# Banded attention: the products of weights and values of the two heads of a pair, one head after the other or alternately

## The chip, the cores and the metric

The kernel runs on 1 core of one Trainium2 chip. The metric is the device time of one execution in microseconds (us); for the kernel before it is given as the median of 3 runs, and every comparison with it is made on the same chip.

## The reference

The program is one block of a first kind (a chunked mLSTM and a "stick-breaking" attention, gates, an MLP) and two layers of a second kind. Each of these two layers computes an HGRN2 recurrence over eight heads of 128 and, beside it, banded attention over sixteen heads of 64 with two key/value heads; the two results, gated, are multiplied by an output matrix. All data are float32; the sequence has 512 rows, the model 1024 columns. What the change touches is the end of the banded attention:

```python
    s = jnp.einsum('bnqkgd,bnskd->bnkgqs', qb, kw).astype(jnp.float32) * ATT_SCALE
    ...
    s = jnp.where(mask[None, :, None, None, :, :], s, NEG_INF)
    ...
    p = jax.nn.softmax(jnp.concatenate([s, sink], axis=-1), axis=-1)[..., :-1]
    o = jnp.einsum('bnkgqs,bnskd->bnqkgd', p.astype(v.dtype), vw)
```

The sequence is cut into four blocks of 128 queries. Block n sees the keys and values of blocks n and n-1, and block 0 its own only.

## The kernel before

`layer` runs once for each of the two layers. It projects the normed input with blocks of 128x512 (`gemm_a`, `gemm_b`, lines 149 to 151 of `mm3`: every product of a float32 matrix is three products of rounded halves), runs the recurrence (`hgrn`), and then the banded attention, two heads at a time, in `swa_pair(p)`, p from 0 to 7. A scheduler orders the whole program: it keeps the order of the program's dependences, gives earlier code and code under `K.above` precedence, and fixes the order of each engine's instructions when the program is built. Pairs 0 to 3 stand under `K.above(p2)`, ahead of the last projections `proj_qa(1)` and `proj_za(1)`; pairs 4 to 7 come after the transposes of the recurrence's result (line 672) and ahead of `wo1`, the first half of the output product. In both places products of lines 149 to 151 lie between the attention's instructions.

`swa_pair` treats its two heads e = 0 and e = 1 in a loop. For each head:

- lines 602 and following: the scores of four blocks on TensorE, into PSUM tiles `xa`;
- line 608 (VectorE: mask and minimum), line 610 (ScalarE: exponential with its sum), lines 614 to 619: the softmax, the sums' inverse multiplied in;
- lines 624 and 626: seven transposes of 128x128 on TensorE into two PSUM tiles `xb`;
- lines 628 and 630: ScalarE copies these into the two pages `pT` (named pg in the profile), taken from the pool `hb`, which has four such pages;
- lines 634 and 636: seven products of values (`va`, 128 rows by 64 columns, the stationary operand) with the transposed weights (128x128, moving) into the head's half of the PSUM tile `xc`: partitions 0 to 63 for e = 0 and 64 to 127 for e = 1.

```python
                for n in range(NT):
                    o = po[r, n * P:(n + 1) * P]
                    nc.tensor.matmul(o, va[0][:, n, vv], pT[n // 2][:, n % 2, 0:P], start=True, stop=(n == 0))
                    if n:
                        nc.tensor.matmul(o, va[0][:, n - 1, vv], pT[(n - 1) // 2][:, (n - 1) % 2, P:2 * P],
                                         start=False, stop=True)
```

After both heads, line 638 multiplies the whole tile `xc` by the gate `zt`, which a DMA of line 586 brought (two pages). `xc` has one buffer. At the layer's end `bcast2` (line 266) loads two broadcast vectors into pages of `hb`, for the output's norm (line 708).

A product of two plain float32 tiles, such as those of lines 634 and 636, is one row in the built order and two matmul records in the profile, called two passes below. So a head's seven products are 14 passes; 16 pairs in two layers make 224 products and 448 passes. `hgrn` also writes parts of PSUM tiles: line 432 uses 32 columns of the array per product, four such groups in turn.

Of the kernel before, what the change touches and what calls it, by code (L numbers as in the profile page):

```python
# [17 lines left out]
P = 128  # L18
S = 512
D = 1024  # L20
NT = S // P
# [297 lines left out]
def layer(K, l, xd, win, wout, gpost, lbp, ghead, sinks, out, gnext):  # L319

    nc, tc = K.nc, K.tc
    if True:
        def page(tag, bufs):
            return K.lp.tile([P, S], F32, name=K.nm("pg"), tag=tag, bufs=bufs)
# [4 lines left out]
        def ha():  # L329
            return page("ha", 4)  # L330

        def hb():
            return page("hb", 4)
# [9 lines left out]
        else:  # L343
            mx = K.lc.tile([P, 8], F32, name="lbm")
            nc.vector.tensor_tensor(mx, lb[:, 0, :], lb[:, 1, :], ALU.max)
            e = K.lc.tile([P, 2, 8], F32, name="lbe")
# [179 lines left out]
        qT, kT, va = {}, [], []  # L526
# [56 lines left out]
        def swa_pair(p):  # L583
            kv = p // 4
            zt = page("zs", 2)
            nc.sync.dma_start(out=zt, in_=za_d[p * P:(p + 1) * P, :])
            po = K.psum("xc", 1)
            for e in range(2):
                h = 2 * p + e
                r = slice(64 * e, 64 * e + 64)  # L590
                pT = [hb().rearrange("p (s t) -> p s t", s=2) for _ in range(2)]
                pn, den = K.small(NT, "pn", 4), K.small(NT, "den", 4)
                Ps = []
                for n in range(NT):
                    w = P if n == 0 else 2 * P
                    if n % 2 == 0:
                        psc = K.psum("xa").rearrange("p (n s) -> p n s", n=2)
                        for i in range(2):
                            wi = P if n + i == 0 else 2 * P
                            t1 = (n + i + 1) * P  # L600
                            for j in range(2):
                                nc.tensor.matmul(psc[:, i, 2 * P - wi:], qT[p][e][:, t1 - P:t1], kT[kv][j][:, t1 - wi:t1],  # L602
                                                 start=(j == 0), stop=(j == 1))
                        prp = ha()
                    sc = psc[:, n % 2, 2 * P - w:]
                    pr = prp[:, n % 2 * 256:n % 2 * 256 + 256]
                    prw = pr[:, 2 * P - w:]
                    nc.vector.tensor_tensor_reduce(prw, sc, K.band[:, 2 * P - w:], 1.0,  # L608
                                                   nsnk[:, h:h + 1], ALU.add, ALU.min, accum_out=pn[:, n:n + 1])
                    nc.scalar.activation(prw, prw, AF.Exp, bias=pn[:, n:n + 1], scale=-1.0,  # L610
                                         accum_out=den[:, n:n + 1])
                    Ps.append((pr, prw))
                es = K.small(NT, "es", 4)
                nc.scalar.activation(es, pn, AF.Exp, bias=snk[:, h:h + 1])
                nc.vector.tensor_tensor(den, den, es, ALU.add)
                nc.vector.reciprocal(den, den)
                for n in range(NT):
                    pr, prw = Ps[n]
                    nc.vector.tensor_scalar(prw, prw, den[:, n:n + 1], None, ALU.mult)
                for i in range(2):  # L620
                    pt = K.psum("xb").rearrange("p (s t) -> p s t", s=2)
                    for s in range(2):
                        sb = 2 * i + s
                        nc.tensor.transpose(pt[:, s, 0:P], Ps[sb][0][:, P:2 * P], K.ident)  # L624
                        if sb + 1 < NT:
                            nc.tensor.transpose(pt[:, s, P:2 * P], Ps[sb + 1][0][:, 0:P], K.ident)
                    if i == 0:
                        nc.scalar.copy(pT[i], pt)
                    else:
                        nc.scalar.copy(pT[i].rearrange("p s t -> p (s t)")[:, :384], pt.rearrange("p s t -> p (s t)")[:, :384])  # L630
                vv = slice(64 * kv, 64 * kv + 64)
                for n in range(NT):
                    o = po[r, n * P:(n + 1) * P]
                    nc.tensor.matmul(o, va[0][:, n, vv], pT[n // 2][:, n % 2, 0:P], start=True, stop=(n == 0))  # L634
                    if n:
                        nc.tensor.matmul(o, va[0][:, n - 1, vv], pT[(n - 1) // 2][:, (n - 1) % 2, P:2 * P],  # L636
                                         start=False, stop=True)
            nc.vector.tensor_tensor(oa[p], po, zt, ALU.mult)

        mark = lambda: tc.cur_priority  # L640
# [22 lines left out]
        with K.above(p2):  # L663
            for p in range(4):
                swa_pair(p)
# [11 lines left out]
        for p in range(4, 8):  # L677
            swa_pair(p)
# [584 lines left out]
```

## Time and profile before

| | us |
|---|---|
| median of 3 runs | 1846.03 (1844.19 to 1846.66) |
| the profiled execution, its own time | 1845.76 |
| its span, first to last instruction | 1844.0 |
| TensorE (PE) busy | 1804.3 (98%) |
| VectorE (DVE) busy | 1083.2 (59%) |
| ScalarE (ACT) busy | 858.3 (47%) |

The span is the time from the first to the last instruction; 1.76 us of the execution's own time lie outside it. A matmul's record begins when it starts to stream and its end is modelled, so records overlap: how long a run of matmuls holds TensorE is read from the starts, from the first of the run to the first of what comes next. In rows of the timeline, xN is the number of records merged into a row.

### The profile page before, as it was taken

To read this page: it belongs to the slowest core of one execution; us is meant where nothing else is said; L and a number is where in the kernel's file an instruction comes from. 1 tells how busy PE (TensorE), PEld (TensorE's weight loads), DVE (VectorE), ACT (ScalarE), POOL (GpSimd) and SP (SyncE) were. 2 spreads that over 40 slices of the span, in tenths; PEclk is the share of its full clock that TensorE was granted. 3 is DMA by queue.
4 is the path that set the end of the run, shared out by engine and by line. 5 is a ranking of instruction groups with operands and counts; after the bars stand their busy time and mean duration, and the time that the engine had idled before them with its cause. 6 is when DMAs were issued, how large, how long until landed. Compare 5 with 4: busy or idle time off the path is not lost.

```text
span 1844.0 us, 29440 instructions
## 1 busy us (share of the span) xinstructions
PE 1804.3 (98%) x11600; PEld 1480.2 (80%) x11600; DVE 1083.2 (59%) x2186; ACT 858.3 (47%) x1701; POOL 170.7 (9%) x223
## 2 busy tenths in 40 slices
PE   7999999999899999999999999999999999999998
PEld 5777788787698888878888888888878888888886
DVE  4365445547555675587474757755365648575733
ACT  4546544343343443355344437565343345375741
POOL 1001011010000110021000001100220000101002
PEclk9999999999999999999999999999999999999999
DMA  7342332221623856387231242222342223322222
GB/s 214 72 103 81 86 92 80 58 92 46 193 95 109 220 125 193 94 220 206 92 119 50 87 132 95 96 86 75 121 154 92 88 75 97 128 86 75 75 69 91
DMA packets 114322, 201.05 MB, mean 109 GB/s; under 512 B 9600, under 2 KB 20224, under 8 KB 114184
## 3 DMA queue, kind: packets, MB, share of 16 engines
q1 hardware_dynamic: 105480, 182.40, 31.8%
q0 software_dynamic: 8704, 16.78, 5.2%
q8 instruction: 91, 1.49, 0.3%
q14 instruction: 47, 0.39, 0.1%
HBM read 184.45 MB, written 14.70 MB: 108 GB/s over the span
## 4 chain that ended last, share of the span: by engine, by line
PE 93%; DMA 3%; ACT 2%; DVE 1%; SPq 0%; issue 0%; POOL 0%; DVEq 0%; POOLq 0%; ACTq 0%
PE mm L150 23%; PE mm L151 23%; PE mm L149 23%; PE xc L634 2%; PE xa L228 2%; PE xa L227 2%; PE xa L229 1%; PE xa L602 1%; PE xc L636 1%; PE mm L227 1%; PE mm L228 1%; PE mm L229 1%; PE xc L1064 1%; PE xa L1046 1%; PE xb L624 1%; PE xc L498 1%
## 5 line engine op out<-in xcount | busy, mean ns | idle before, releaser
L149 PE MATMUL mm<-wh,hh 128*128 128x512 f32 (+1 forms) x896 | 349.0, 390 | 11.7 <-DVE qd L1132 4.6
L138 DVE TENSOR_TENSOR wl<-wr,wh 128x1024 fp32r<-128x1024 f32 (+1 forms) x240 | 288.6, 1211 | 116.5 <-PE mm L150 71.4
L150 PE MATMUL mm<-wl,hh 128*128 128x512 f32 (+1 forms) x896 | 348.7, 389 | 0.8 <-DVE wl L138 0.8
L151 PE MATMUL mm<-wh,hl 128*128 128x512 f32 (+1 forms) x896 | 347.3, 391 | 0.0
L137 ACT CAST wh<-wr 128x1024 fp32r<-128x1024 f32 (+1 forms) x240 | 246.6, 1038 | 123.2 <-PE mm L151 58.2
L149 PE MATMUL mm<-hh,wh 128*128 128x512 f32 x640 | 254.0, 397 | 1.4 <-ACT pg L801 1.4
L151 PE MATMUL mm<-hh,wl 128*128 128x512 f32 x640 | 252.6, 395 | 1.8 <-DVE wl L138 1.7
L150 PE MATMUL mm<-hl,wh 128*128 128x512 f32 x640 | 252.1, 394 | 0.0
L149 PEld LDWEIGHTS mm<-wh,hh 128*128 128x128 f32 x896 | 169.6, 189 | 46.7 <-DVE qd L1132 5.0
L150 PEld LDWEIGHTS mm<-wl,hh 128*128 128x128 f32 x896 | 169.4, 189 | 34.2 <-DVE wl L138 2.4
L151 PEld LDWEIGHTS mm<-wh,hl 128*128 128x128 f32 x896 | 168.0, 189 | 31.6 <-DVE hl L259 0.7
L151 PEld LDWEIGHTS mm<-hh,wl 128*128 128x128 f32 x640 | 120.2, 188 | 28.8 <-DVE wl L138 3.0
L149 PEld LDWEIGHTS mm<-hh,wh 128*128 128x128 f32 x640 | 120.2, 188 | 27.3 <-ACT pg L801 2.7
L150 PEld LDWEIGHTS mm<-hl,wh 128*128 128x128 f32 x640 | 120.4, 188 | 24.5
L115 POOL TENSOR_TENSOR sm<-sm,nhalf 128x4 f32<-128x4 f32 (+1 forms) x64 | 59.1, 923 | 506.4 <-DVE sm L507 329.8
L149 PE MATMUL mm<-qd,wh 128*128 128x512 f32 (+1 forms) x288 | 105.5, 366 | 0.0
L150 PE MATMUL mm<-qd,wh 128*128 128x512 f32 (+1 forms) x288 | 105.4, 366 | 0.0
L151 PE MATMUL mm<-qd,wl 128*128 128x512 f32 (+1 forms) x288 | 105.2, 365 | 0.0
L610 ACT ACTIVATE pg<-pg,sm 128x256 f32<-128x256 f32 (+1 forms) x128 | 60.9, 478 | 15.5 <-DVE sm L608 15.4
L1146 DVE TENSOR_TENSOR hr<-hr 128x512 f32<-128x512 f32 (+1 forms) x36 | 22.7, 631 | 69.4 <-ACT hr L1145 68.8
L149 PEld LDWEIGHTS mm<-qd,wh 128*128 128x128 f32 x288 | 54.3, 189 | 8.8
L151 PEld LDWEIGHTS mm<-qd,wl 128*128 128x128 f32 x288 | 54.3, 189 | 8.7
(312 smaller groups left out, 3061.1 us busy)
## 6 DMA issues: line engine op xcount, KB each, us to landing
wr<-in_w_in_dram SPq DMA_DIRECT2D x160, 512.0 KB, 4.8
wr<-in_w_out_dram SPq DMA_DIRECT2D x40, 512.0 KB, 3.6
wr<-in_w_up_dram SPq DMA_DIRECT2D x32, 512.0 KB, 6.3
wr<-in_w_down_dram SPq DMA_DIRECT2D x32, 512.0 KB, 5.8
wx<-in_w_down_dram POOLq DMA_DIRECT2D x24, 512.0 KB, 9.4
wx<-in_w_down_dram SPq DMA_DIRECT2D x8, 512.0 KB, 3.5
wr<-in_w_down_dram POOLq DMA_DIRECT2D x8, 512.0 KB, 8.1
zh<-pg SPq DMA_DIRECT2D x16, 256.0 KB, 2.1
```

Source lines behind the costliest of these rows:

```text
L115: self.nc.gpsimd.tensor_tensor(y, ms, e, ALU.pow)
L137: nc.scalar.copy(hi, raw)
L138: nc.vector.tensor_tensor(lo, raw, hi.bitcast(F32), ALU.subtract)
L149: nc.tensor.matmul(ps, sh, mh, start=(k == 0), stop=False)
L150: nc.tensor.matmul(ps, sh, ml, start=False, stop=False)
L151: nc.tensor.matmul(ps, sl, mh, start=False, stop=(k == n - 1))
L227: nc.tensor.matmul(ps, ah, wh, start=(first and k == 0), **kw)
L228: nc.tensor.matmul(ps, ah, wl, start=False, **kw)
L229: nc.tensor.matmul(ps, al, wh, start=False, **kw)
L610: nc.scalar.activation(prw, prw, AF.Exp, bias=pn[:, n:n + 1], scale=-1.0, accum_out=den[:, n:n + 1])
L634: nc.tensor.matmul(o, va[0][:, n, vv], pT[n // 2][:, n % 2, 0:P], start=True, stop=(n == 0))
L1146: nc.vector.tensor_tensor(r[:, m, t], r[:, m, t], r[:, m, t], ALU.mult)
```

## The change

The loop over the two heads only collects the pages `pT` of each head in `pTs`. Behind it, one loop issues the products of both heads, block by block, e = 0 and e = 1 in turn, into the same halves of `xc` as before. Number, shape and operands of all products stay as they were. (The products that were on lines 634 and 636 are all on line 638 in the changed kernel; lines from 638 on stand two lower.)

```diff
             po = K.psum("xc", 1)
+            pTs = []
             for e in range(2):
                 h = 2 * p + e
-                r = slice(64 * e, 64 * e + 64)
                 pT = [hb().rearrange("p (s t) -> p s t", s=2) for _ in range(2)]
...
-                vv = slice(64 * kv, 64 * kv + 64)
-                for n in range(NT):
-                    o = po[r, n * P:(n + 1) * P]
-                    nc.tensor.matmul(o, va[0][:, n, vv], pT[n // 2][:, n % 2, 0:P], start=True, stop=(n == 0))
-                    if n:
-                        nc.tensor.matmul(o, va[0][:, n - 1, vv], pT[(n - 1) // 2][:, (n - 1) % 2, P:2 * P],
-                                         start=False, stop=True)
+                pTs.append(pT)
+            vv = slice(64 * kv, 64 * kv + 64)
+            for n in range(NT):
+                for k in ((n,), (n, n - 1))[n > 0]:
+                    for e in range(2):
+                        o = po[64 * e:64 * e + 64, n * P:(n + 1) * P]
+                        w = slice((n - k) * P, (n - k + 1) * P)
+                        nc.tensor.matmul(o, va[0][:, k, vv], pTs[e][k // 2][:, k % 2, w],
+                                         start=(k == n), stop=(k < n or n == 0))
             nc.vector.tensor_tensor(oa[p], po, zt, ALU.mult)
```

**Place 1.** TensorE, the first pair of the first layer; pg1667 and pg1668 are the pages of head e = 0, pg1678 and pg1679 those of e = 1. Before:

```order
L634 MATMUL xc1666_10090<-pg1667_10091,pg1432_8415 64x128 x2
L636 MATMUL xc1666_10090<-pg1667_10091,pg1432_8415 64x128
L634 MATMUL xc1666_10090<-pg1668_10092,pg1432_8415 64x128
L636 MATMUL xc1666_10090<-pg1667_10091,pg1432_8415 64x128
L634 MATMUL xc1666_10090<-pg1668_10092,pg1432_8415 64x128
L636 MATMUL xc1666_10090<-pg1668_10092,pg1432_8415 64x128
L634 MATMUL xc1666_10090<-pg1678_10141,pg1432_8415 64x128 x2
L636 MATMUL xc1666_10090<-pg1678_10141,pg1432_8415 64x128
L634 MATMUL xc1666_10090<-pg1679_10142,pg1432_8415 64x128
L636 MATMUL xc1666_10090<-pg1678_10141,pg1432_8415 64x128
L634 MATMUL xc1666_10090<-pg1679_10142,pg1432_8415 64x128
L636 MATMUL xc1666_10090<-pg1679_10142,pg1432_8415 64x128
```

In the changed kernel (the first eight of the fourteen):

```order
L638 MATMUL xc1666_10090<-pg1667_10091,pg1432_8415 64x128
L638 MATMUL xc1666_10090<-pg1678_10134,pg1432_8415 64x128
L638 MATMUL xc1666_10090<-pg1667_10091,pg1432_8415 64x128
L638 MATMUL xc1666_10090<-pg1678_10134,pg1432_8415 64x128
L638 MATMUL xc1666_10090<-pg1667_10091,pg1432_8415 64x128
L638 MATMUL xc1666_10090<-pg1678_10134,pg1432_8415 64x128
L638 MATMUL xc1666_10090<-pg1668_10092,pg1432_8415 64x128
L638 MATMUL xc1666_10090<-pg1679_10135,pg1432_8415 64x128
```

Before, all seven products of one head stand ahead of the other's seven; now the pages alternate from row to row, in one run of fourteen.

**Place 2.** TensorE, the second pair; pg1691 and pg1692 belong to e = 0, pg1702 and pg1703 to e = 1. Before:

```order
L626 MATMUL xb1712_10283<-ident_75,pg1709_10264 128x128
L536 MATMUL mt1639_9891<-ident_75,pg1633_9847 128x128 x4
L634 MATMUL xc1690_10194<-pg1691_10195,pg1432_8415 64x128 x2
L636 MATMUL xc1690_10194<-pg1691_10195,pg1432_8415 64x128
L634 MATMUL xc1690_10194<-pg1692_10196,pg1432_8415 64x128
L636 MATMUL xc1690_10194<-pg1691_10195,pg1432_8415 64x128
L634 MATMUL xc1690_10194<-pg1692_10196,pg1432_8415 64x128
L636 MATMUL xc1690_10194<-pg1692_10196,pg1432_8415 64x128
L624 MATMUL xb1712_10283<-ident_75,pg1709_10264 128x128
L602 MATMUL xa1732_10363<-qd1431_8414,qd1486_8733 128x256 x4
L151 MATMUL mm1636_9861<-wh1624_9782,hl1115_6286 128x512
L634 MATMUL xc1690_10194<-pg1702_10245,pg1432_8415 64x128 x2
```

In the changed kernel, the rows where head e = 0 ends its transposes:

```order
L624 MATMUL xb1712_10276<-ident_75,pg1709_10257 128x128
L626 MATMUL xb1712_10276<-ident_75,pg1709_10257 128x128
L624 MATMUL xb1712_10276<-ident_75,pg1709_10257 128x128
L638 MATMUL xc1690_10194<-pg1691_10195,pg1432_8415 64x128
L602 MATMUL xa1732_10356<-qd1431_8414,qd1486_8733 128x256 x4
L150 MATMUL mm1636_9861<-wl1628_9789,hh1113_6284 128x512
L151 MATMUL mm1636_9861<-wh1627_9788,hl1115_6286 128x512
L149 MATMUL mm1636_9861<-wh1627_9788,hh1113_6284 128x512
```

and, some rows further, where the run begins:

```order
L150 MATMUL mm1640_9900<-wl1622_9777,hh1112_6283 128x512
L638 MATMUL xc1690_10194<-pg1702_10238,pg1432_8415 64x128
L638 MATMUL xc1690_10194<-pg1691_10195,pg1432_8415 64x128
L638 MATMUL xc1690_10194<-pg1702_10238,pg1432_8415 64x128
L638 MATMUL xc1690_10194<-pg1691_10195,pg1432_8415 64x128
L638 MATMUL xc1690_10194<-pg1702_10238,pg1432_8415 64x128
L638 MATMUL xc1690_10194<-pg1692_10196,pg1432_8415 64x128
L624 MATMUL xb1724_10331<-ident_75,pg1720_10308 128x128
L626 MATMUL xb1724_10331<-ident_75,pg1720_10308 128x128
L638 MATMUL xc1690_10194<-pg1703_10239,pg1432_8415 64x128
```

Before, e = 0 had its run of seven right behind its transposes. Now its first product (block 0) stands there alone, and the other thirteen wait for e = 1 and stand alternately, here with two transposes of the next pair in between (six and seven).

**Place 3.** TensorE, the sixth pair, where few products of lines 149 to 151 are left between; pg1810 and pg1811 are the pages of e = 1. Before:

```order
L150 MATMUL mm1887_11035<-wl1882_11000,hh1762_10505 128x512
L634 MATMUL xc1798_10670<-pg1810_10721,pg1432_8415 64x128 x2
L636 MATMUL xc1798_10670<-pg1810_10721,pg1432_8415 64x128
L624 MATMUL xb1832_10807<-ident_75,pg1828_10784 128x128
L626 MATMUL xb1832_10807<-ident_75,pg1828_10784 128x128
L624 MATMUL xb1832_10807<-ident_75,pg1828_10784 128x128
L626 MATMUL xb1832_10807<-ident_75,pg1830_10794 128x128
L672 MATMUL mt1771_10550<-ident_75,pg1591_9573 128x128 x4
L151 MATMUL mm1886_11009<-wh1881_10999,hl1764_10507 128x512
L151 MATMUL mm1887_11035<-wh1881_10999,hl1764_10507 128x512
L634 MATMUL xc1798_10670<-pg1811_10722,pg1432_8415 64x128
L636 MATMUL xc1798_10670<-pg1810_10721,pg1432_8415 64x128
```

In the changed kernel:

```order
L602 MATMUL xa1840_10832<-qd1431_8414,qd1616_9767 128x256 x4
L149 MATMUL mm1886_11009<-wh1881_10999,hh1762_10505 128x512
L150 MATMUL mm1886_11009<-wl1882_11000,hh1762_10505 128x512
L149 MATMUL mm1887_11035<-wh1881_10999,hh1762_10505 128x512
L150 MATMUL mm1887_11035<-wl1882_11000,hh1762_10505 128x512
L674 MATMUL mt1771_10550<-ident_75,pg1591_9573 128x128 x4
L151 MATMUL mm1886_11009<-wh1881_10999,hl1764_10507 128x512
L151 MATMUL mm1887_11035<-wh1881_10999,hl1764_10507 128x512
L638 MATMUL xc1798_10670<-pg1810_10714,pg1432_8415 64x128
L638 MATMUL xc1798_10670<-pg1799_10671,pg1432_8415 64x128
L638 MATMUL xc1798_10670<-pg1810_10714,pg1432_8415 64x128
L638 MATMUL xc1798_10670<-pg1799_10671,pg1432_8415 64x128
```

Before, the first three products of e = 1 came right behind four products of lines 149 and 150 (the last of them is shown); now scores, products, a transpose of line 674 (672 before) stand between the last transpose of e = 1 and the run of both heads.

Over a layer, the products of lines 634 and 636 stand in 22 runs before: one of 14 (pair 0), seven of 7, seven of 4 and seven of 3 products. In the changed kernel there are 18: one of 14, four of 13, three of 7, three of 6, and seven single products. Of the DMA queue (SP), in each layer two loads of the output matrix (line 133) move ahead of the two loads of line 266; the rest of the queue stands as before.

## Rows read from the trace of the kernel before

**Rows 1.** The page: busy time by engine, and the chain that ended last.

```profile
PE 1804.3 (98%) x11600; PEld 1480.2 (80%) x11600; DVE 1083.2 (59%) x2186; ACT 858.3 (47%) x1701; POOL 170.7 (9%) x223
...
PE 93%; DMA 3%; ACT 2%; DVE 1%; SPq 0%; issue 0%; POOL 0%; DVEq 0%; POOLq 0%; ACTq 0%
```

**Rows 2.** TensorE's waits from 1100 to 1345 us: us in total, times, longest.

```profile
PE xa L602 <- DVE sm L608: 0.7, 1, 0.7
PE mm L149 <- ACT hh L675: 0.7, 1, 0.7
PE xc L634 <- DVE pg L638: 0.4, 1, 0.4
```

**Rows 3.** TensorE's timeline, two runs of the first layer: start, us, instruction.

```profile
1174.61 0.65 PE L634 MATMUL xc<-pg,pg 128*64 128x128 f32 x4
1175.09 0.38 PE L636 MATMUL xc<-pg,pg 128*64 128x128 f32 x2
1175.31 0.38 PE L634 MATMUL xc<-pg,pg 128*64 128x128 f32 x2
...
1176.28 0.33 PE L624 MATMUL xb<-ident,pg 128*128 128x128 f32 x1
...
1177.25 0.65 PE L634 MATMUL xc<-pg,pg 128*64 128x128 f32 x4
1177.73 0.38 PE L636 MATMUL xc<-pg,pg 128*64 128x128 f32 x2
1178.05 0.33 PE L624 MATMUL xb<-ident,pg 128*128 128x128 f32 x1
```

**Rows 4.** TensorE's timeline, pair 0 of the first layer, both heads.

```profile
1166.84 0.65 PE L634 MATMUL xc<-pg,pg 128*64 128x128 f32 x4
...
1168.20 0.27 PE L636 MATMUL xc<-pg,pg 128*64 128x128 f32 x1
1168.25 0.27 PE L634 MATMUL xc<-pg,pg 128*64 128x128 f32 x1
1168.31 0.27 PE L636 MATMUL xc<-pg,pg 128*64 128x128 f32 x1
1168.36 0.27 PE L634 MATMUL xc<-pg,pg 128*64 128x128 f32 x1
...
1169.66 0.44 PE L602 MATMUL xa<-qd,qd 128*128 128x128 f32 x2
```

**Rows 5.** TensorE's timeline, line 432: four groups of 32 columns in turn.

```profile
918.39 0.55 PE L432 MATMUL xa<-qx,qd 128*32 128x48 f32 x32
918.87 0.50 PE L150 MATMUL mm<-hl,wh 128*128 128x512 f32 x1
```

**Rows 6.** Weight loads by line: minimum, median, maximum ns; first and last start.

```profile
L634 PEld LDWEIGHTS xc<-pg,pg x256: 132/137/137, 1166.8 to 1770.4; 128*64 128x64 f32 x128
...
L432 PEld LDWEIGHTS xa<-qx,qd x512: 106/110/113, 918.4 to 1540.6; 128*32 128x32 f32 x171
```

**Rows 7.** Stretches: length, busy us (records) by engine, granted clock, DMA share, GB/s.

```profile
1166.00:1215.00 49.00, 49.00 (x301) 40.46 (x300) 28.80 (x77) 23.89 (x61) 5.54 (x3) 1.00 0.22 73
1232.00:1264.00 32.00, 31.60 (x221) 26.01 (x221) 21.61 (x88) 22.32 (x71) 0.00 (x0) 1.00 0.06 18
1724.00:1756.00 32.00, 31.60 (x223) 26.38 (x224) 21.61 (x86) 22.54 (x71) 0.00 (x0) 1.00 0.06 18
```

**Rows 8.** Timelines of TensorE and ScalarE, pair 4 of the first layer, head e = 1.

```profile
1240.45 0.27 PE L624 MATMUL xb<-ident,pg 128*128 128x128 f32 x1
...
1240.48 0.59 ACT L628 COPY pg<-xb 128x512 f32<-128x512 f32 x1 [1.38 <-PE xb L626]
...
1241.47 0.47 ACT L630 COPY pg<-xb 128x384 f32<-128x384 f32 x1
...
1242.49 0.65 PE L634 MATMUL xc<-pg,pg 128*64 128x128 f32 x4
```

**Rows 9.** The queue's loads of line 266, and the first use of what they bring.

```profile
1273.51 0.83 SPq L266 DMA_DIRECT2D pg<-in_g_post_dram x2
...
1308.55 1.29 POOL L708 TENSOR_TENSOR qd<-qd,pg 128x512 f32<-128x512 f32 x1 [116.24 <-ACT pg L706]
```

## The prediction

> **What bounds the kernel now.** I read the page first. TensorE is busy for 98% of the span and carries 93% of the chain that ended last [rows 1]; the other engines are near half. The table of waits then says what TensorE waits for in the stretch that holds the whole attention of the first layer: three waits, 1.8 us together in 245 us, one of them in front of the products that the change moves [rows 2]. The second layer has the same three waits. So what TensorE is spared there shortens the span, unless the engines that feed it fall behind. The reader is to see in the rows that TensorE is full, and then to ask what one pass of these products costs it.
>
> **What one pass costs.** A run of 14 passes (a head's seven products) begins at 1174.61 and the next matmul at 1176.28: 1.67 us. A run of 6 passes begins at 1177.25 and the next at 1178.05: 0.80 us [rows 3]. The difference, 0.87 us for 8 passes, is 0.109 us a pass; what is left, 0.80 - 6 x 0.109 = 0.146 us, is paid once per run, on the way into half the array's columns and out again. A run of 8 passes then costs 1.02 us.
>
> Before, by the count of runs in the built order, a layer pays: pair 0, both heads in one run, 2.82 us (1166.84 to 1169.66, [rows 4]); seven runs of 7 products, 7 x 1.67 = 11.69; seven of 4, 7 x 1.02 = 7.14; seven of 3, 7 x 0.80 = 5.60. Together 27.25 us, in two layers 54.5 us, 3% of the span.
>
> **Do two halves overlap?** The trace of before answers it, because pair 0 issues its two heads back to back. Serially its 28 passes would take 28 x 0.109 + 0.146 = 3.20 us; they took 2.82. In the middle single passes begin at 1168.20, 1168.25, 1168.31 and 1168.36, 0.05 to 0.06 us apart, half of 0.109 [rows 4]. That is where the second head's products had caught up with the rest of the first head's. A second sign: 32 passes of line 432, in four groups of 32 columns in turn, hold TensorE for 0.48 us, 0.015 us each [rows 5], although each streams 48 columns, and at the price of a pass of 128 columns (0.109 us) 48 columns are 0.041 us. So groups of columns work at the same time, with plain float32 operands, and with the order that issues them in turn.
>
> The weight loads must keep up. A load of 64 columns is 137 ns long, one of 32 columns 110 ns [rows 6]: 27 ns for 32 columns, so 54 ns for 64. If all loads went one after the other they would allow a pass every 0.054 us, the same as two halves at 0.109 us. This sets no lower step, but no room is left below it either.
>
> The Trainium skill ("TensorE: Matmul & The Clock Gate", Part 3, The mechanism) speaks against this: a weight load overlaps a matmul in flight only where the two use different groups of rows, and both halves here use all 128 rows. By that rule a pass would keep at least its own 0.109 us and the change would gain nothing, which is the second rival below. The trace disagrees: at 1168.20 to 1168.36 full-row passes of 64 columns start 0.05 to 0.06 us apart [rows 4].
>
> **The change, part by part.** With the halves in step, a joint run costs 0.109 us for each pass of its longer half, and 0.146 us. Per layer, by the new order's runs:
> - one run of 14 products (7 each half, 14 passes): 1.67 us;
> - four of 13 (the longer half has 7): 4 x 1.67 = 6.68;
> - three of 7 (4 and 3): 3 x 1.02 = 3.06;
> - three of 6 (3 and 3): 3 x 0.80 = 2.40;
> - seven single products, which pay for a run of their own: 7 x (2 x 0.109 + 0.146) = 2.55.
>
> Together 16.36 us, in two layers 32.7 us. TensorE is spared 54.5 - 32.7 = 21.8 us. If the halves stay staggered by half a step, each of the 11 joint runs of a layer is 0.054 us longer, 1.2 us in all: 20.6 us. I take 21.
>
> What is moved past what. On TensorE the first head's products stand later, behind the second head's softmax; no engine needs them before line 638, which waited for the second head anyway. On ScalarE the copies of lines 628 and 630 need pages of `hb`. All four now stay taken until the joint run, while before the first head's two came free earlier. In the new order the next pair's transposes stand with or behind the end of the joint run (place 3 in the section on the change), so the page is free about when its copy can be made: I cost it at nothing in the sum, and it is the third rival's cause. On the queue two loads of line 266 go behind two weight loads; they were issued at 1273.51 and first used at 1308.55 [rows 9]. A cover of 35 us against a few us: nothing. The gate's load and `xc` are released by line 638 as before.
>
> **What comes back.** Where projections lie between the heads (1166 to 1215), VectorE is busy 28.80 of 49 us and ScalarE 23.89 [rows 7]: they follow. In pairs 4 to 6 little lies between: from 1232 to 1264 VectorE is busy 21.61 and ScalarE 22.32 of 32 us, in the second layer about the same [rows 7]. There a pair's softmax is a chain of short steps on both. Before, pairs 4, 5 and 6 hold TensorE for 3.49, 3.49 and 3.64 us by the prices above, and 2.18, 2.18 and 2.03 after: 4.2 us a layer are spared in this stretch, 8.4 us in two. The stretch would shrink to 27.8 us, with VectorE at 78% and ScalarE at 80%, not full; but a chain with such shares waits at times. The bounds: nothing comes back (21 us gained), or all 8.4 us (12.6 us). No row prices it in between; I take half, 4 us, because both engines keep a fifth of their time free.
>
> So 21 - 4 = 17 us from the profiled execution's 1845.8 us (span 1844.0): 1828.8. The median of the runs is 0.27 us above that execution: **1829 us**.
>
> **The rivals.**
> 1. *The feeders decide*: TensorE reaches the transposes and products sooner, and waits for lines 608 to 630 in most pairs, so that half of the 21 us return. For it: the shares above, and that the order was laid out when the program was built and doesn't adapt. Against: TensorE hardly waits now [rows 2], and 14 to 40 rows of projections lie between many heads. 1845.8 - 10 = 1836 us.
> 2. *The change doesn't overlap*: passes stay 0.109 us apart, as the skill's rule has it. 448 x 0.109 + 36 runs x 0.146 = 54.1 us against 54.5: 1845.6 us, no change. Against it stand the single passes of pair 0.
> 3. *Slower, by the joint wait*: the run of both heads stands behind the second head's two copies, and the next pair's copies behind that run, since no page of `hb` is free; TensorE stands once per pair. The price is the stretch from the second head's last transpose to its products: 1240.45 + 0.27 to 1242.49, 1.8 us in pair 4, of which the copies alone (to the end of line 630 at 1241.94) are 1.2 us [rows 8]. Fully exposed in 16 pairs: 28 us. 1845.8 + 28 - 21 = 1853 us. It decides from 21/16 = 1.3 us a pair. Against: other rows stand between the last transpose and the run in nearly all pairs of the new order, as in place 3.
>
> **How the numbers follow.** Forecast 0.70, first rival 0.18, second 0.08, third 0.04. The predicted time is the forecast's, 1829 us. Its own range goes from nothing given back, and the runs' fixed part partly overlapped as well (1845.8 - 24 = 1822), to all of the 8.4 us given back and the stagger (1834). To hold 8 in 10, I take in the first rival and reach to 1839. A measurement of this kernel can tell about 0.2%, 3.7 us, from no change. Faster than that: the forecast and the first rival, 0.88. Within it: the second rival, 0.08. Slower: the third, 0.04.
>
> **What would show it.** In the changed kernel's timeline, the run of pair 0 should last about 1.7 us in place of 2.82, with starts 0.05 to 0.06 us apart all through it; a lone first product should cost about 0.36 us. The granted clock should stay at 1.00 in these stretches, as now [rows 7]. The waits of TensorE between 1100 and 1345 us should grow from 1.8 us to some 4 us, for lines 608, 628 and 630. The prediction is wrong if the starts stay 0.109 us apart (second rival), or if waits in front of the joint run exceed 1 us a pair (third), or if line 602 and the transposes wait for VectorE or ScalarE in the stretches with projections too (first).

## The result, and the profile after

The changed kernel takes 1820.84 us, median of 4 runs (1820.33 to 1821.88), against 1846.35 us before in the same comparison; the ratio is 0.9859, interval 0.9837 to 0.9880. That is 25.5 us less, faster, as forecast, but 8 us below the 1829 us forecast, and just below the range (1822 to 1839). The profiled execution took 1821.35 us (span 1819.6), 24.4 us less than that of before.

The page, busy time by engine [rows 1]:

```profile
PE 1781.9 (98%) x11600; PEld 1460.7 (80%) x11600; DVE 1081.0 (59%) x2186; ACT 856.0 (47%) x1701; POOL 168.7 (9%) x223
...
PE 92%; DMA 3%; ACT 2%; DVE 2%; issue 0%; SPq 0%; POOL 0%; DVEq 0%; POOLq 0%; ACTq 0%
```

TensorE is as full as it was, in a shorter span. Its waits from 1100 to 1345 us [rows 2]:

```profile
PE xa L602 <- DVE sm L608: 0.7, 1, 0.7
PE mm L149 <- ACT hh L677: 0.6, 1, 0.6
PE mm L149 <- DVE pg L706: 0.3, 1, 0.3
```

1.6 us, where 1.8 us were before and some 4 us were forecast: nothing came back as waiting. TensorE's timeline, three runs of the products, now on line 638 [rows 3, 4]:

```profile
1165.78 1.75 PE L638 MATMUL xc<-pg,pg 128*64 128x128 f32 x28
1167.46 0.33 PE L602 MATMUL xa<-qd,qd 128*128 128x128 f32 x1
...
1172.96 0.43 PE L638 MATMUL xc<-pg,pg 128*64 128x128 f32 x2
1173.32 0.39 PE L602 MATMUL xa<-qd,qd 128*128 128x256 f32 x1
...
1191.44 1.74 PE L638 MATMUL xc<-pg,pg 128*64 128x128 f32 x26
1193.12 0.33 PE L624 MATMUL xb<-ident,pg 128*128 128x128 f32 x1
```

Pair 0 holds TensorE from 1165.78 to 1167.46, 1.68 us in place of 2.82: 28 passes of 0.06 us. A single first product costs 0.36 us, a run of 13 (here of a later pair) 1.68. The same timeline, cut down to the first 0.02 us of pair 0:

```profile
1165.78 0.33 PE L638 MATMUL xc<-pg,pg 128*64 128x128 f32 x2
```

Two passes begin together. Read one record at a time, the starts are 1165.78 and 1165.79, 1165.94 and 1165.95, 1166.05 and 1166.06 us, and so on: each half starts a pass every 0.109 us, as before, and the two halves go in step, not half a step apart. Summed over all runs, from each run's start to the next matmul's, the products hold TensorE for 32.8 us in place of 54.5. The sum of the prediction said 32.7 (and 21.8 us spared, of which it took 21 for a stagger).

The stretch from the first to the last of them, by the weight loads of lines 636 before and 638 after (columns as in [rows 6]). Before:

```profile
L636 PEld LDWEIGHTS xc<-pg,pg x192: 137/137/137, 1167.2 to 1770.7; 128*64 128x64 f32 x192
```

After:

```profile
L638 PEld LDWEIGHTS xc<-pg,pg x448: 132/137/138, 1165.8 to 1746.3; 128*64 128x64 f32 x150
```

Before, the first load (line 634) was at 1166.8 [rows 6] and the last at 1770.7: 603.9 us. Now it is 580.5 us, 23.4 less. 21.7 of them are the products; the other 1.7 lie around them. Layer by layer, from the first product's start to that of the matmul behind the last one, with the same matmuls in between, it is 112.6 us before and 100.7 after: 23.8 us less in the two layers, while the time between them grew by 0.5. 1.0 us of the 24.4 was won ahead of the first product, in code that the change leaves alone; in the kernels below that first product starts anywhere between 1166.3 and 1169.9 us, so this is scatter.

The stretch of pairs 4 to 6, shifted and shortened by 4 us [rows 7]:

```profile
1226.00:1254.00 28.00, 28.00 (x225) 23.18 (x224) 22.22 (x87) 23.49 (x76) 0.00 (x0) 1.00 0.06 20
```

VectorE is at 79%, ScalarE at 84%, near what the prediction worked out for a stretch that had shrunk (78% and 80%). TensorE is busy for all of its 28 us. The granted clock stayed at 1.00, the level of 2.4 GHz.

### The profile page after: what moved, and what is told of

The parts are those of the page before. It is cut to its first block, busy times and chain, and to the rows that moved or that the text cites. A ratio compares the mean times of both kernels' runs of the same rounds, so it can differ in the third digit from the quotient of the medians.

```text
span 1819.6 us, 29429 instructions
## 1 busy us (share of the span) xinstructions
PE 1781.9 (98%) x11600; PEld 1460.7 (80%) x11600; DVE 1081.0 (59%) x2186; ACT 856.0 (47%) x1701; POOL 168.7 (9%) x223
## 4 chain that ended last, share of the span: by engine, by line
PE 92%; DMA 3%; ACT 2%; DVE 2%; issue 0%; SPq 0%; POOL 0%; DVEq 0%; POOLq 0%; ACTq 0%
PE mm L151 23%; PE mm L150 23%; PE mm L149 23%; PE xc L638 2%; PE xa L602 2%; PE xa L228 1%; PE xa L227 1%; PE xa L229 1%; PE mm L227 1%; PE mm L228 1%; PE mm L229 1%; PE xc L1066 1%; PE xa L1048 1%; PE xb L624 1%; PE xc L498 1%; PE xa L443 1%
```

## The experiments

Two questions are open: whether the gain is the overlap of the halves alone, or in part the move of the products behind the second head; and why nothing came back. All kernels below start from the changed one. In the first four, `body` is the product with its operands, unchanged.

**The move without the alternation.**

```diff
-            for n in range(NT):
-                for k in ((n,), (n, n - 1))[n > 0]:
-                    for e in range(2):
+            for e in range(2):
+                for n in range(NT):
+                    for k in ((n,), (n, n - 1))[n > 0]:
                         body
```

> The products of both heads stand behind both softmaxes, as in the change, but all seven of head 0 ahead of all seven of head 1, so that the halves do not alternate. Overlap alone (theory): 26 runs a layer instead of 22, 0.109 us a pass and 0.146 us a run as before: the products hold TensorE for about 56 us in two layers (54.5 before), the time is 1845 to 1849 us. The move and the new order bring a part (rival; the change gained 24 us where the products were spared 21.7): 1843 us or less, with the same products' time of 54 to 57 us.

Measured: 1847.96 us against 1846.04 before, ratio 1.0013 (1.0005 to 1.0022). The products hold TensorE for 55.7 us in 52 runs. Pair 0 in its timeline:

```profile
1168.98 2.89 PE L638 MATMUL xc<-pg,pg 128*64 128x128 f32 x28
1171.80 0.61 PE L602 MATMUL xa<-qd,qd 128*128 128x128 f32 x3
```

The same 28 records take 2.82 us, as before the change. So the move and the new order by themselves bring nothing: the time is 2 us longer, with 1.2 us more in the products and eight more runs. All of the gain needs turns between the halves.

**Turns of two products.**

```diff
             for n in range(NT):
-                for k in ((n,), (n, n - 1))[n > 0]:
-                    for e in range(2):
+                for e in range(2):
+                    for k in ((n,), (n, n - 1))[n > 0]:
                         body
```

> As the change, but the heads take turns by blocks of queries: both products of a block for head 0 (four passes), then both for head 1. If TensorE takes up the other half's passes from some rows ahead (theory), a run of 13 products costs the same 1.67 us as in the change, and the time is 1820 to 1822 us. If passes start strictly in the order issued (rival), each turn overlaps in one pass only: a run of 13 takes 21 steps of 0.109 in place of 14, 2.4 us, and 16 pairs add 12 us: about 1833 us.

Measured: 1821.88 us, ratio 0.9870 (0.9857 to 0.9884), with the products at 33.5 us. A run of 13 products:

```profile
1178.47 1.74 PE L638 MATMUL xc<-pg,pg 128*64 128x128 f32 x26
1180.14 0.33 PE L624 MATMUL xb<-ident,pg 128*128 128x128 f32 x1
```

1.67 us, the same as in the change, where the expectation's estimate for starts in the order issued was 2.4 us. So TensorE does not need strict turns: with four passes for one half and four for the other it takes them up in parallel. The Trainium skill ("TensorE: Matmul & The Clock Gate", Part 3, The mechanism) has matmuls start in strict program order. The trace disagrees, and so did that of the kernel before: there the pass of line 634 at 1168.25 us [rows 4] can only be one of head 1, since head 0 ends with two passes of line 636, and it starts ahead of head 0's last one, at 1168.31.

There is a limit, though: with turns of 14 passes, as in pair 0 of the experiment above, only 0.38 of a possible 1.5 us overlaps. Read one record at a time, the second head's first pass starts there when three of the first head's fourteen are still to start, and so it does in pair 0 of the kernel before. Turns between four and fourteen passes were not tested.

**Without the single products.** In the built order of the change seven products a layer stand alone, ahead of their run, because the first one needs only head 0.

```diff
-                    for e in range(2):
+                    for e in (1, 0):
```

> As the change, with head 1 ahead of head 0 within each turn: the first product of a pair then waits for the second head, and no single product stands alone ahead of the run (11 runs a layer in place of 18). Theory (TensorE is the bound, and a run pays 0.146 us of its own): 14 single products at 0.36 us go, the products hold TensorE for 27.6 us in place of 32.8, and the time is about 1815.7 us. Rival (VectorE and ScalarE now set the pace in pairs 4 to 7): 1819 to 1821 us, and TensorE waits for lines 608 to 630.

Measured: 1815.61 us, ratio 0.9834 (0.9821 to 0.9848). The products hold TensorE for 27.8 us in 22 runs; TensorE's waits between 1100 and 1345 us are 1.4 us. So a run has a price of its own: 14 of them gone are 5 us of the time in which the products hold TensorE, and the kernel goes from 1820.84 to 1815.61 us.

That is not the whole price. A run of four products of the kernel before, with the matmuls ahead of it and behind it:

```profile
1181.76 0.39 PE L149 MATMUL mm<-wh,hh 128*128 128x512 f32 x1
1181.99 0.39 PE L150 MATMUL mm<-wl,hh 128*128 128x512 f32 x1
1182.30 0.43 PE L634 MATMUL xc<-pg,pg 128*64 128x128 f32 x2
...
1183.32 0.33 PE L624 MATMUL xb<-ident,pg 128*128 128x128 f32 x1
1183.49 0.27 PE L626 MATMUL xb<-ident,pg 128*128 128x128 f32 x1
1183.60 0.27 PE L624 MATMUL xb<-ident,pg 128*128 128x128 f32 x1
```

From line 149 to line 150 the start moves on by 0.23 us, from line 150 to the run by 0.31. Behind the run the first step is 0.17 us, the second 0.11. Neither of the two longer steps lies between the run's first start and the next matmul's. Against the median steps of the same shapes, these borders come to 0.16 to 0.18 us a run: 7.2 us in the 44 runs before (a wait in front of line 634 left out), 5.9 in the 36 of the change, 4.1 in the 22 here. The two attention stretches, with the same matmuls in all three kernels, take 225.3, 201.5 and 194.1 us: 7.3 less here than in the change, 5.0 of them in the products. The profiled executions differ by 3.8 us only, because here the first product starts 4.1 us later, in code that is the same.

**One run per pair.** Besides, the blocks go in falling order, so that the first product needs the last of the copies.

```diff
-            for n in range(NT):
+            for n in reversed(range(NT)):
                 for k in ((n,), (n, n - 1))[n > 0]:
-                    for e in range(2):
+                    for e in (1, 0):
```

> As the kernel with head 1 ahead, and the blocks of queries in falling order, so that the first product needs the last copy: 8 runs of 14 products a layer. Theory (TensorE bound): 16 x 1.67 = 26.7 us for the products, 6 us less than in the change, 1814.8 us. Rival (the later start exposes the last copy, or the feeders set the pace): 1817 us or more, with TensorE waiting in front of the runs.

Measured: 1813.49 us, ratio 0.9824 (0.9811 to 0.9838); the products hold TensorE for 26.9 us in 16 runs. Its waits from 1100 to 1345 us:

```profile
PE xa L602 <- DVE sm L608: 0.7, 1, 0.7
PE mm L149 <- ACT hh L677: 0.6, 1, 0.6
```

No run waits for the last copy. This kernel is 32.6 us below the kernel before and 7 us below the change. Against the kernel with single products gone the 2 us are within the two intervals; its attention stretches take 192.7 us, 1.4 less. ScalarE is busy for 24.41 us of the 28 from 1226 to 1254 (87%), VectorE for 24.39, and still no wait is added.

**More work for the feeders.** The prediction took 4 us off because VectorE and ScalarE would be near 80% in pairs 4 to 6. The next kernels give VectorE one more multiplication by 1.0, in the chain between the softmax and the transposes, for two of the four blocks of a head, and for all four; the change itself ran beside them.

```diff
                     nc.vector.tensor_scalar(prw, prw, den[:, n:n + 1], None, ALU.mult)
+                    if n % 2:
+                        nc.vector.tensor_scalar(prw, prw, 1.0, None, ALU.mult)
```

(For all four, without the condition.)

> The change itself once more, beside the two kernels with more work on VectorE: 1820 to 1822 us.

> The change, and for two of the four blocks of each head one more multiplication by 1.0 on VectorE, in the chain between the softmax and the transposes: 64 more instructions of up to 0.35 us, 22 us; in the stretch of pairs 4 to 6, some 10 of them, which would take VectorE from 22.2 of 28.0 us to 25.5 (91%). If the feeders have room to spare (theory), the time is within 2 us of the change: up to 1823 us. If they already set the pace near 80% (rival: the reason for the 4 us that the prediction took off), each head is 0.5 to 0.7 us later and TensorE waits: 1826 us or more.

> The same for all four blocks of each head: 128 more instructions, up to 44 us; in the stretch of pairs 4 to 6 VectorE would be busy for 28.5 of 28.0 us. Both theories expect a loss here: with room up to full use (theory), the stretch grows by 1 to 3 us a layer, 1823 to 1828 us; with feeders that already set the pace near 80% (rival), by the whole 6 us a layer: 1833 us or more.

Measured: the change 1822.55 us, half a us above what was expected of it (ratio 0.9871, 0.9853 to 0.9889), two blocks 1823.06 us (0.9870, 0.9850 to 0.9889), four blocks 1822.01 us (0.9866, 0.9850 to 0.9882). All three are the same. In the kernel with four, the added instructions (line 620), by shape:

```profile
L620 DVE TENSOR_SCALAR pg<-pg 128x256 f32<-128x256 f32 x96 | 23.7, 288 | 0.1
L620 DVE TENSOR_SCALAR pg<-pg 128x128 f32<-128x128 f32 x32 | 7.1, 222 | 0.0
```

and the stretch of pairs 4 to 6, which the wait table follows (1100 to 1345 us):

```profile
1226.00:1254.00 28.00, 28.00 (x226) 23.44 (x225) 26.60 (x118) 21.95 (x71) 0.00 (x0) 1.00 0.08 20
```

```profile
PE xa L602 <- DVE sm L608: 0.7, 1, 0.7
PE mm L149 <- ACT hh L678: 0.6, 1, 0.6
```

30.8 us of work were added, VectorE is busy for 26.60 of 28 us (95%), and TensorE still doesn't wait there (one step ahead of the layer's last run, at 1266.5 us, is 0.27 us longer than usual, and the table does not list it). The rival falls; and the theory's own number for four blocks, a loss of 1 to 3 us a layer, was missed as well. One thing limits the test: the scheduler lays out a new order for each kernel, and in the one with four it spread the products of lines 149 to 151 differently between the steps of the last pairs. So what was shown is that VectorE at 95% costs nothing in an order made for it, not that it would cost nothing in the change's own order. ScalarE was given no extra work.

## Why the prediction was wrong, point by point

- **What bounds the kernel**: right. TensorE was and stays full, and what it was spared came out of the span.
- **What one pass costs, and what a run costs**: right for a pass, too small for a run. 0.109 us a pass and 0.146 us a run gave the time in which the products hold TensorE: 32.7 us for the change (measured 32.8), 27.6 for the kernel without single products (27.8) and 26.7 for the one with whole runs (26.9). But 0.146 us leaves out the longer steps ahead of a run and behind it, some 0.16 us more. With 36 runs in place of 44 that is 1.3 us that the sum did not have.
- **Do two halves overlap?** Right: 0.06 us a pass over the whole run of pair 0, against 0.10 before. The stagger of half a step, worth 1.2 us in the sum, did not appear: the starts come in pairs, two within 0.01 us, and not 0.05 to 0.06 us apart all through the run, as the prediction's sign had it. Nor do weight loads go one after the other, as its estimate of a load had supposed: those of the two halves start within 0.01 us of each other too. The second rival (no overlap, 1845.6 us) is refuted, and for two halves of the columns so is the rule of the Trainium skill that the prediction cites beside it.
- **What is moved past what**: right. The copies, the pages of `hb` and the loads of line 266 cost nothing that a wait shows. The third rival (slower, 1853 us) is refuted by the wait table: no run of line 638 stands in it, neither in the change nor in the kernel whose runs all wait for the last copy.
- **What comes back**: this step failed. "No row prices it in between; I take half, 4 us" and the first rival (half of all, 1836 us) rested on the shares of VectorE and ScalarE. The shares came out near what was worked out, 79% and 84%, and the price was zero: waits of 1.6 us after, 1.8 before, where the sign was some 4 us for lines 608, 628 and 630. Even the wait in front of line 634 [rows 2] is gone. A busy share below full did not mean a loss here. In the built order of these pairs the scores and transposes of the next head stand between a head's steps, which would hide the chain; that this is the reason is argued, not tested. Without the deduction, and with the 21.7 us measured, the sum is 1845.8 - 21.7 + 0.3 = 1824.4 us, which lies in the range: to fall below it took the next point as well.
- **The rest**, some 3.5 us to the 1820.84 us measured: 1.7 us around the products, which the sum had no term for; 1.0 us of scatter ahead of them; 0.8 us because the profiled execution after lies 0.5 us above its median, where the sum put it 0.3 below. The first is 2.1 us less in the two attention stretches and 0.5 us more between them. The 2.1 us are two things, as far as steps from start to start can tell: 1.3 us at the borders of eight fewer runs, and 0.9 us of the wait in front of line 634, 0.47 us a layer when read from the starts (0.4 in the wait table). The kernels with 22 and 16 runs bear out the borders: beyond the products, their attention stretches lose another 2.3 and 2.9 us.
- **The range**: its low end of 1822 us rested on "the runs' fixed part partly overlapped", which no run showed, and it left no room for scatter. The repeat of the change, 1822.55 us, lies inside it; the first median does not.

## What to carry to other kernels

Where TensorE is full and products use half its columns, issue them alternately into both halves: here 224 products then hold it for 33 us in place of 54.5. Look at the built order afterwards for products that stand alone: each run in half the columns has a price (0.146 us here, and some 0.16 us in the steps beside it), and to begin with the operand that is ready last kept the runs together (another 7 us). Do not take off time merely because other engines will be busier; look in the wait table for a wait that would grow. Here there was none, and nothing came off.

## What was not expected of the hardware

TensorE took up products of the other half ahead of earlier ones when the turns were four passes long (1.67 us a run, as with strict turns), but hardly when they were fourteen (2.82 us for 28 passes, 0.38 us less than in series; there only the last three passes of the first half were overtaken). And VectorE, in line ahead of TensorE's transposes, could be loaded from 79% to 95% of a stretch with no wait of TensorE in it.
